# Down projections by seven block products beside a fixed order of the gate and up stage

## The chip, the core and the metric

The kernel runs on one core of a Trainium2 chip. The metric is the device time in microseconds of one execution. TensorE (PE) multiplies, VectorE (DVE) and ScalarE (ACT) split operands and take results out of PSUM, GpSimd (POOL) does some elementwise work and issues DMAs from a queue of its own, and SyncE (SP) issues the other DMAs.

## What is computed

Two layers over 768 tokens (256 of context, 512 latent) of 1024 features. Each layer is a SwiGLU half-step, a mixer, and a second SwiGLU half-step. In the second layer the context is needed up to the mixer's keys and values only, so that six sub-layers s = 0 to 5 run: SwiGLU on 768 tokens (s = 0, 2, 3), the two mixers (s = 1, 4), and SwiGLU on 512 tokens (s = 5).

```python
D_MODEL, SEQ, CTX_LEN, DEPTH, D_FF = 1024, 512, 256, 2, 2816

def _ffn_sublayer(h, shift, scale, gate, g_pre, g_post, w_gate, w_up, w_down):
    u = _modulate(_rmsnorm(h, g_pre), shift, scale)          # h * (1 + scale) + shift
    y = (jax.nn.silu(u @ w_gate) * (u @ w_up)) @ w_down
    return h + FFN_RES * gate * _rmsnorm(y, g_post)
...
for l in range(DEPTH):
    x  = _ffn_sublayer(x, ...);  xc = _ffn_sublayer(xc, ...)
    u  = _modulate(_rmsnorm(x, norm_pre[l, 1]), mod[:, 3], mod[:, 4])
    uc = _modulate(_rmsnorm(xc, norm_pre[l, 1]), mod_c[3], mod_c[4])
    y, yc = _even_mixer(...) if l % 2 == 0 else _odd_mixer(...)
    x = x + mod[:, 5] * _rmsnorm(y, norm_post[l, 1])
    x = _ffn_sublayer(x, ...)
    if not last: xc = the same for the context
return x
```

## The kernel before

**Products.** Every float32 product is made of three passes: an operand is split into hi (its leading bits, a copy by ACT) and lo (the rest, a subtraction by DVE), and hi*hi, hi*lo and lo*hi are accumulated in PSUM. `halves` (L191 to L196) makes the two parts; `weights` (L177) does so for a block of 1024 columns, 512 at a time.

**A SwiGLU sub-layer** (`ffn`, L527) works on two chunks of tokens, of n = 384 each for s = 0, 2 and 3. It has three parts.

- The first two of the 22 tiles of 128 features are plain products (`products`).
- *Gate and up*: the other twenty features, two tiles at a time, by seven products (`strassen`, L588; Strassen's scheme in Winograd's form). There are ten pairs p, each with a job for gate (b = 0) and one for up (b = 1), so twenty jobs. A job loads two blocks of weights, makes four sums of them on DVE (L614 to L617), splits seven blocks of 512 columns, and issues 84 matmuls of 384 columns (L601). ACT copies partial results out of PSUM (L629) and DVE adds (L634) and multiplies (L638). A pair of finished tiles h goes to DRAM (`hd`, L658).
- *Down*: `type2` (L665) per chunk c. For each of the 22 feature tiles it loads 1024 columns of the weights (L193 splits them) and 384 columns of h (`lhs`, L576, `hilo`, L721), and `t2mm` (L694) issues 18 matmuls of 512 columns for three tiles of 128 tokens (L701): three passes, two halves of D. The last four feature tiles (STAG = 4) are done token tile by token tile, 24 matmuls each, so that a token tile is finished while the next is still multiplied.

**The boundary** (`boundary`, L494). For a finished token tile, the squares (L505) and the product with the gate (L506) read PSUM. The rest, x += G * rms(y) (L514), the norm (`normed`, L407: L410, L414), the transposes on TensorE (`turned`, L416, L419) and the split of u (L395, L393, L193), is run at once for the second chunk, and for the first chunk beside the second chunk's products (`later`, L671). Where the next sub-layer uses seven products, `Sums` (L422) makes what they need of u; `prepare` (L430) has GpSimd add hi and lo of the first chunk again (L437).

**Order.** A scheduler puts the instructions of each engine in order, by the order of the program and a model of when operands are ready; each engine then runs its list strictly in order. `late` (L81) keeps an instruction behind those that were issued before it. s = 5 (`joint`) takes all four token tiles at a time in its down projection and is otherwise alike. The modulation (`ada_steps`, L104) runs step by step beside the jobs of s = 0 and the mixers.

## Time and profile before

| what | us |
|---|---|
| three runs | 2631.05, 2623.03, 2626.58 (median 2626.58) |
| span of the profiled execution | 2636.3 |
| TensorE busy, of this span | 2546.2 |
| VectorE busy | 1757.5 |
| ScalarE busy | 1351.8 |
| GpSimd busy | 325.3 |
| down projection of s = 0, first matmul to last of the first chunk | 392.8 to 485.3 |
| and of the second chunk | 485.1 to 582.4 |

The profiled execution is one run; its span is 9.7 us longer than the median of the runs. Matmuls are pipelined and overlap in the profile, so a busy TensorE says that matmuls are in flight, and the distance from one matmul to the next says how fast they go.

### The profile page before, as it was taken

How to read it: one execution, taken by the hardware profiler on the slowest of the kernel's cores; microseconds unless marked ns; L12 is line 12 of the kernel's file. 1: busy time of each engine (PE TensorE's matmuls, PEld its weight loads, DVE VectorE, ACT ScalarE, POOL GpSimd, SP SyncE). 2: the span in 40 equal slices, each digit the busy share in tenths (PEclk: the TensorE clock that was granted, in tenths of full speed). 3: DMA queues.
4: the chain of work that ended last, by engine and by line, in shares of the span. 5: the costliest groups of instructions: out<-in, count | busy, mean ns of one | idle time of the engine just before them, and what ended most of it. 6: DMA issues, size and time to landing. Idle time of an engine off the chain costs nothing.

```text
span 2636.3 us, 38740 instructions
## 1 busy us (share of the span) xinstructions
PE 2546.2 (97%) x13980; PEld 2237.5 (85%) x13980; DVE 1757.5 (67%) x3199; ACT 1351.8 (51%) x2783; POOL 325.3 (12%) x356
## 2 busy tenths in 40 slices
...
PEclk8999999999999999999999999999999999999999
DMA  7445436541387443232555332235554552544542
GB/s 275 144 160 168 152 127 206 192 160 53 119 293 266 157 141 96 96 105 100 187 184 189 124 97 95 98 107 177 198 181 152 200 176 82 177 135 128 161 167 88
DMA packets 147761, 403.00 MB, mean 153 GB/s; under 512 B 16504, under 2 KB 33576, under 8 KB 147568
## 3 DMA queue, kind: packets, MB, share of 16 engines
...
q14 instruction: 84, 0.69, 0.1%
HBM read 351.91 MB, written 48.55 MB: 152 GB/s over the span
## 4 chain that ended last, share of the span: by engine, by line
PE 80%; DVE 7%; issue 5%; ACT 3%; POOL 3%; DMA 2%; POOLq 0%; DVEq 0%; ACTq 0%; SPq 0%
PE px L601 17%; PE py L601 12%; PE pz L601 12%; PE d110a L701 4%; PE d100a L701 4%; PE d000a L701 4%; PE d010a L701 4%; PE ada L122 3%; PE d001a L701 3%; PE d101a L701 3%; PE eo0a L701 1%; PE oq1a L701 1%; PE qkv1a L701 1%; PE opT L1286 1%; PE gu L201 1%
## 5 line engine op out<-in xcount | busy, mean ns | idle before, releaser
L210 POOL TENSOR_TENSOR b_0pr<-b_0pv,mhalf 128x1 f32<-128x1 f32 x4 | 2.2, 560 | 983.9 <-DVE b_0pv L208 983.9
L634 DVE TENSOR_TENSOR cp<-px,cp 128x384 f32<-128x384 f32 (+1 forms) x160 | 76.5, 520 | 56.3 <-PE px L601 56.3
L724 ACT ACTIVATE hh<-hr 128x384 fp32r<-128x384 f32 x132 | 68.6, 521 | 81.5 <-DMA hr<-hd 80.6
L725 DVE TENSOR_TENSOR hh<-hr,hh 128x384 fp32r<-128x384 f32 x132 | 72.9, 559 | 50.6 <-ACT hh L724 49.5
L636 ACT ACTIVATE h<-cp 128x384 f32<-128x384 f32 (+1 forms) x160 | 77.0, 498 | 26.1 <-DVE cp L634 21.9
L122 PE MATMUL ada<-wa,sc 128*32 128x512 f32 x512 | 83.8, 611 | 0.5 <-DVE cols L137 0.4
L634 DVE TENSOR_TENSOR cp<-pz,cp 128x384 f32<-128x384 f32 (+1 forms) x80 | 41.9, 524 | 57.4 <-PE pz L601 56.4
L638 DVE TENSOR_TENSOR h<-cp,h 128x384 f32<-128x384 f32 (+1 forms) x160 | 79.6, 519 | 0.4
L629 ACT ACTIVATE cp<-px 128x384 f32<-128x384 f32 (+1 forms) x160 | 71.4, 446 | 0.0
L634 DVE TENSOR_TENSOR cp<-py,cp 128x384 f32<-128x384 f32 (+1 forms) x80 | 41.7, 521 | 26.7 <-PE py L601 17.2
L614 DVE TENSOR_TENSOR w<-w,w 128x512 f32<-128x512 f32 x80 | 56.8, 709 | 1.6 <-DMA w<-in_wgu_dram 0.2
L193 DVE TENSOR_TENSOR d110w_0lo<-d110w,d110w_0hi 128x512 fp32r<-128x512 f32 x22 | 15.2, 691 | 63.6 <-ACT d110w_0hi L193 63.6
L617 DVE TENSOR_TENSOR w<-w,w 128x512 f32<-128x512 f32 x80 | 55.3, 691 | 2.0
L615 DVE TENSOR_TENSOR w<-w 128x512 f32<-128x512 f32 x80 | 55.2, 690 | 1.9
L616 DVE TENSOR_TENSOR w<-w,w 128x512 f32<-128x512 f32 x80 | 55.1, 689 | 1.5
L701 PE MATMUL d011a<-d011w_0hi,hh 128*128 128x512 f32 x132 | 52.7, 399 | 0.2 <-ACT hh L724 0.2
L701 PE MATMUL d101a<-d101w_0hi,hh 128*128 128x512 f32 x132 | 52.5, 398 | 0.0
L701 PE MATMUL d001a<-d001w_0hi,hh 128*128 128x512 f32 x132 | 52.5, 398 | 0.0
L701 PE MATMUL d100a<-d100w_512hi,hh 128*128 128x512 f32 x132 | 52.4, 397 | 0.0
L701 PE MATMUL d000a<-d000w_512hi,hh 128*128 128x512 f32 x132 | 52.4, 397 | 0.0
L701 PE MATMUL d010a<-d010w_0hi,hh 128*128 128x512 f32 x132 | 52.3, 396 | 0.0
L701 PE MATMUL d101a<-d101w_512hi,hh 128*128 128x512 f32 x132 | 52.2, 396 | 0.0
...
## 6 DMA issues: line engine op xcount, KB each, us to landing
w<-in_wgu_dram SPq DMA_DIRECT2D x175, 512.0 KB, 3.5
...
wa<-in_w_ada_dram SPq DMA_DIRECT2D x42, 512.0 KB, 4.3
d000w<-in_w_down_dram SPq DMA_DIRECT2D x22, 512.0 KB, 3.5
d001w<-in_w_down_dram SPq DMA_DIRECT2D x22, 512.0 KB, 3.8
d010w<-in_w_down_dram SPq DMA_DIRECT2D x22, 512.0 KB, 3.9
```

The costliest lines, as they stand in the source:

```text
L122: ins = nc.tensor.matmul(acc[32 * g:32 * g + 32, :], lhsT=self.sc[:, k, :], rhs=raws[g], start=(k == 0), stop=(k == KD - 1), skip_group_ch ...
L601: mm = lambda x, y, **kw: nc.tensor.matmul(out, lhsT=x, rhs=y, skip_group_check=True, **kw)
L614: nc.vector.tensor_sub(x3, x1, x3)
L615: nc.vector.tensor_add(x1, x1, x2)
L617: nc.vector.tensor_sub(x4, x4, x2)
L629: nc.scalar.activation(t, src, AF.Copy)
L634: nc.vector.tensor_add(t, acc, t)
L636: nc.scalar.activation(hc, t, AF.Silu)
L638: nc.vector.tensor_mul(hc, t, hc)
L701: mm(acc[:, h:min(h + 512, n)], lhsT=x[xi][:, js], rhs=w[h // 512][wi], start=(k == 0 and xi == 0 and wi == 0), stop=(k == nk - 1 and xi = ...
L724: self.nc.scalar.activation(t[:, 0], src, AF.Copy)
L725: self.nc.vector.tensor_sub(t[:, 1], src, t[:, 0].bitcast(F32))
```

## The change

The change has five parts, for s = 0, 2 and 3 where nothing else is said.

1. *Down by seven products* (`down`). The features are taken as eleven pairs of tiles, the tokens as two chunks and D as two halves of 512. The sums of h (`h_sums`) and of the weights (`down_sums`) are made during gate and up and go to DRAM: `hd` has four blocks for a pair instead of two, and the new `wt` holds sums of the weights. `down_load` and `down_sums` load and store the weights on GpSimd's queue, in the two tiles that the gate uses later. `down` then runs seven products in turn, each over eleven feature tiles; loads and splits are made for two feature tiles at a time, four ahead (AHEAD). PSUM is taken out by `keep`, `left`, `right`, `right2` and `left2`.
2. *Gate and up in a fixed order*. `chain` ties each instruction of ACT and DVE in this stage (and of ACT, DVE and SP in `down`) to the one before it in the program. The weights of a job are made one job ahead, in the steps of the generator `made`. Splits are of 1024 columns, and the results of two chunks are taken in one instruction of 768 columns.
3. *The joint sub-layer* (s = 5) uses the same jobs without the fixed order; its down projection stays as it was.
4. *The boundary* is cut into halves of D and into two steps, norm (`rest`) and transposes (`make_u`), which are placed apart. `Sums.prepare` goes; the float32 tiles of u are kept.
5. *Storage*. Four slots of 1024 columns hold hi and lo, instead of eight of 512; blocks of 512 take a whole slot, too. The scratch for the DMAs of GpSimd's queue is set to 8192.

Cut to its core:

```diff
+    def chain(self, last, ins):
+        e = ins.ins.engine
+        if e in last:
+            self.tc.add_manual_dep(ins.ins, last[e], mybir.DependencyInfo(
+                mybir.DependencyClass.NoSync, mybir.DependencyReason.DATA), reason="chain")
+        last[e] = ins.ins.name
...
+    def wtiles(self, n, name, one=False):
+        return [self.ws.tile([P, n], F32R, tag=("o" if one else "w") + e, bufs=2 if one else 4, name=name + e) for e in ("hi", "lo")]
...
+        if sums is not None and c == 0:
+            ut = sums.first[j] = [self.c3([P, 4, P], F32, f"{name}b{h}") for h in range(2)]
...
-        def prepare(self):
...
+        def half(i, y):
+            nc.scalar.activation(self.junk(f"{name}{i}")[:, cut[i]], y, AF.Square, accum_out=ss[:, i:i + 1])
+            nc.vector.tensor_mul(y1[:, cut[i]], y, g[:, cut[i]])
+        def end():
+            nc.vector.tensor_add(ss[:, 0:1], ss[:, 0:1], ss[:, 1:2])
+            r = self.rms_r(ss[:, 0:1], D, name + "p")
+            def rest():
+                x = bp.tile([P, D], F32, tag="bx", bufs=2, name=name + "x")
+                nc.gpsimd.dma_start(x, xsrc(t))
...
+                    self.normed(x, y1, name + "u")
+            return rest, lambda: nxt and self.make_u(y1, t, *nxt, name + "u")
...
+    def down_load(self, l, s, p):
+        b = [self.bp.tile([P, D], F32, tag=f"G{e}", name=f"wt{l}{s}{p}{e}") for e in range(2)]
+        for e in range(2):
+            self.late(self.nc.gpsimd.dma_start(b[e], self.a["w_down"][l, s, (2 * p + e) * P:(2 * p + e + 1) * P, :]))
+        return b
+    def down_sums(self, b, wt, chain):
+        nc = self.nc
+        (b11, b12), (b21, b22) = ((x[:, 0:512], x[:, 512:]) for x in b)
+        chain(nc.vector.tensor_add(b11, b11, b12))
+        chain(nc.vector.tensor_add(b12, b12, b22))
+        self.late(nc.gpsimd.dma_start(wt[0], b[0]))
+        chain(nc.vector.tensor_add(b22, b11, b22))
+        chain(nc.vector.tensor_add(b21, b22, b21))
+        self.late(nc.gpsimd.dma_start(wt[1], b[1]))
+    def h_sums(self, h, n, hd, nm, joint, chain=lambda ins: ins):
+        nc = self.nc
+        a11, a21, a12, a22 = (x[:, c * n:(c + 1) * n] for x in h for c in range(2))
+        nc.sync.dma_start(hd[1], h[1])
...
+        s12 = self.bp.tile([P, 2, n], F32, tag="by", bufs=3, name=f"hs{nm}")
+        s4 = self.junk(f"hs{nm}")[:, 0:n]
+        chain(nc.vector.tensor_sub(s12[:, 0], a22, a21))
+        chain(nc.vector.tensor_sub(a21, a11, a21))
+        nc.sync.dma_start(hd[0], h[0])
+        minus = lambda out, x, y: chain(nc.vector.scalar_tensor_tensor(out, x, -1.0, y, op0=ALU.mult, op1=ALU.subtract))
+        minus(s12[:, 1], s12[:, 0], a11)
+        nc.sync.dma_start(hd[2], s12.rearrange("p c n -> p (c n)"))
+        minus(s4, s12[:, 1], a12)
+        nc.sync.dma_start(hd[3][:, 0:n], s4)
+    def down(self, l, s, n, hd, wt, g, start, finish, hook):
...
+        def make():
+            i, p, a, b = todo.pop(0)
...
+            w = min(2, np_ - p)
+            q = slice(p, p + w)
+            ar = self.c3([P, w, n], F32, f"dh{nm}")
+            chain(nc.sync.dma_start(ar, a(q)))
+            tag, bufs = ("bx", 2) if i < 5 and p // 2 % 3 == 2 else ("raw", 3)
+            br = self.ws.tile([P, w, 512], F32, tag=tag, bufs=bufs, name=f"dw{nm}")
+            chain(nc.sync.dma_start(br, b(q)))
+            ah, al = (self.c3([P, w, n], F32R, f"dh{nm}{e}") for e in "hl")
+            halves(ah, al, ar)
+            bh, bl = (t.rearrange("p (e n) -> p e n", e=w) for t in self.wtiles(w * 512, f"dw{nm}s"))
+            halves(bh, bl, br)
...
+        def run():
...
+            parts = {q: e for q, e in (((5, 0), (0, 0)), ((5, 2), (1, 0)), ((5, 6), (0, 1)), ((5, 7), (2, 0)), ((5, 9), (1, 1)), ((6, 1), (2, 1)))}
...
+                a = min(k + self.AHEAD, len(steps) - 1, (i + 1) * np_ + 1 if p > np_ - 4 else len(steps))
+                while todo and steps[a] not in ready:
+                    make()
...
+                end = np_ - (5 if i == len(jobs) - 1 else 3)
+                if p == 0 or end <= p < np_ - 1:
+                    continue
+                for j in range(m):
+                    for e in held:
+                        mms(acc[j], e, j, first)
+                    if p == np_ - 1:
+                        done(j, acc[j])
+                held = []
...
+            for xi, wi in ((0, 0), (0, 1), (1, 0)):
+                nc.tensor.matmul(out, lhsT=x[xi][:, js], rhs=w[wi], start=first and p == 0 and xi == wi,
...
+        def left(j, acc):
+            chain(nc.vector.tensor_add(k12[:, 0, j], acc, k12[:, 0, j]))
+            ends[0, j] = start(0, j, g)
+            ends[0, j][0](0, k12[:, 0, j])
+        def right(j, acc):
+            minus(k12[:, 1, j], acc)
+            ends[0, j][0](1, k12[:, 1, j])
+            finish(0, j, ends[0, j][1])
+        def right2(j, acc):
+            minus(u5[:, j], acc)
+            ends[1, j] = start(1, j, g)
+            ends[1, j][0](1, u5[:, j])
+        def left2(j, acc):
+            ends[1, j][0](0, acc)
+            finish(1, j, ends[1, j][1])
+        x, z = bank("dx"), []
+        product(blk(0, 0), raw(0, 0), x, True, keep(k12[:, 0]))
+        product(blk(1, 0), raw(1, 0), lambda: bank("dy"), True, left)
+        product(blk(2, 1), mod(1, 1), x, False, keep(k12[:, 1]))
+        product(blk(2, 0), mod(0, 0), lambda: z.extend(bank("dy")) or z, True, keep(u5))
+        product(blk(3, 0), raw(1, 1), lambda: z, False, right)
+        product(blk(0, 1), mod(0, 1), x, False, right2)
+        product(blk(1, 1), mod(1, 0), x, False, left2)
...
+        chain = (lambda ins: ins) if joint else lambda ins: self.chain(last, ins)
...
+            w["a11"], w["a12"] = cut(split(r1, nm + "a1"))
+            w["a22"] = split(r2[:, 512:], nm + "a22", True)
+            yield w
...
+            chain(nc.vector.tensor_sub(x3, x1, x3))
+            chain(nc.vector.tensor_add(x1, x1, x2))
+            chain(nc.vector.tensor_add(x2, x3, x2))
+            chain(nc.vector.tensor_sub(x4, x4, x2))
+            yield
+            w["s1"], w["s2"] = cut(split(r2, nm + "s12"))
+            yield
+            w["s3"], w["s4"] = cut(split(r1, nm + "s34"))
+            yield
...
+            (u1, u2), (u4, u5) = ([t[:, c] for c in range(2)] for t in cp)
+            product(x, w["a11"], b11, True)
+            copy(u1, x)
+            after = step()
+            product(y, w["a12"], b21, True)
+            chain(nc.vector.tensor_add(u1, y, u1))
+            step()
+            product(z, w["s1"], t1, True)
+            copy(u5, z)
+            product(x, w["s2"], t2, False)
+            copy(u2, x)
+            step()
+            product(z, w["s4"], b22, False)
+            chain(nc.vector.tensor_add(u2, z, u2))
+            out(0)
+            step()
+            product(y2, w["a22"], t4, True)
+            copy(u4, y2)
+            between()
+            product(x, w["s3"], t3, False)
+            chain(nc.vector.tensor_add(cp[1], x.unsqueeze(1).to_broadcast([P, 2, n]), cp[1]))
+            out(1)
...
+            if joint or (b and p != NF // 2 - 2):
+                return
+            r = p - 1 + b if p < NF // 2 - 1 else p
+            self.down_sums(wb, wt[r], chain)
+            if r < NF // 2 - 1:
+                wb = self.down_load(l, s, r + 1)
...
+        parts = dict(zip(range(1, 8), [(0, 0), (1, 0), None, (0, 1), (2, 0), (1, 1), (2, 1)] if len(ts) > 2 else
+                         [(0, 0), (1, 0), None, None, (0, 1), None, (1, 1)])) if ts else {}
...
+    nc = _bacc.Bacc("TRN2", target_bir_lowering=False, num_devices=1, dynamic_dma_scratch_size=8192)
```

**VectorE in gate and up of s = 2.** The rows are DVE's around the start of the job for p = 4, b = 0; names with 0140 are this job's weights, `cp01300` and the like the results of a job, `w` the loaded weights. Before:

```order
L193 TENSOR_TENSOR 0140a11lo_10461<-w01400_10456,0140a11hi_10460 128x512
L614 TENSOR_TENSOR w01400_10456<-w01401_10458,w01400_10456 128x512
L615 TENSOR_TENSOR w01401_10458<-w01401_10458 128x512
L193 TENSOR_TENSOR 0140a12lo_10465<-w01400_10456,0140a12hi_10464 128x512
L634 TENSOR_TENSOR cp01310_10354<-py00131_10350,cp01310_10354 128x384
L193 TENSOR_TENSOR 0140a22lo_10469<-w01401_10458,0140a22hi_10468 128x512
L638 TENSOR_TENSOR h01_6_10174<-cp01310_10354,h01_6_10174 128x384
L616 TENSOR_TENSOR w01401_10458<-w01400_10456,w01401_10458 128x512
L617 TENSOR_TENSOR w01400_10456<-w01400_10456,w01401_10458 128x512
L193 TENSOR_TENSOR 0140s1lo_10477<-w01401_10458,0140s1hi_10476 128x512
L193 TENSOR_TENSOR 0140s2lo_10481<-w01401_10458,0140s2hi_10480 128x512
```

After, where 0140 is made during the job before:

```order
L796 TENSOR_TENSOR 0140a1lo_9794<-w01400_9789,0140a1hi_9793 128x1024
L796 TENSOR_TENSOR 0140a22lo_9798<-w01401_9791,0140a22hi_9797 128x512
L846 TENSOR_TENSOR cp01310_9774<-py00131_9770,cp01310_9774 128x384
L809 TENSOR_TENSOR w01400_9789<-w01401_9791,w01400_9789 128x512
L810 TENSOR_TENSOR w01401_9791<-w01401_9791 128x512
L811 TENSOR_TENSOR w01401_9791<-w01400_9789,w01401_9791 128x512
L812 TENSOR_TENSOR w01400_9789<-w01400_9789,w01401_9791 128x512
L796 TENSOR_TENSOR 0140s12lo_9845<-w01401_9791,0140s12hi_9844 128x1024
L854 TENSOR_TENSOR cp01310_9774<-pz00131_9772,cp01310_9774 128x384
L839 TENSOR_TENSOR h01_6_9635<-cp01310_9774,h01_6_9635 128x768
L796 TENSOR_TENSOR 0140s34lo_9863<-w01400_9789,0140s34hi_9862 128x1024
L861 TENSOR_TENSOR cp01311_9775<-px00131_9773,cp01311_9775 128x768
```

The splits are wider, the two additions from py and pz stand at fixed places among them, and the multiplication of a feature tile is one row of 768 columns.

**VectorE from gate and up to down of s = 2.** The names `d010w` (before), `dh010` and `dw010` (after) are the down projection's operands; `cp01101` and `h01_20` belong to the last job. Before:

```order
L193 TENSOR_TENSOR 01101s4lo_12303<-w011010_12274,01101s4hi_12302 128x512
L193 TENSOR_TENSOR 01101s3lo_12307<-w011010_12274,01101s3hi_12306 128x512
L634 TENSOR_TENSOR cp011000_12176<-px001100_12175,cp011000_12176 128x384
L634 TENSOR_TENSOR cp011001_12177<-px001100_12175,cp011001_12177 128x384
L193 TENSOR_TENSOR d010w0_0lo_12428<-d010w0_12425,d010w0_0hi_12427 128x512
L193 TENSOR_TENSOR d010w0_512lo_12432<-d010w0_12425,d010w0_512hi_12431 128x512
L634 TENSOR_TENSOR cp011010_12314<-py001101_12310,cp011010_12314 128x384
L193 TENSOR_TENSOR d010w1_0lo_12461<-d010w1_12458,d010w1_0hi_12460 128x512
L638 TENSOR_TENSOR h01_20_12134<-cp011010_12314,h01_20_12134 128x384
```

After:

```order
L861 TENSOR_TENSOR cp011001_11528<-px001100_11526,cp011001_11528 128x768
L846 TENSOR_TENSOR cp011010_11656<-py001101_11652,cp011010_11656 128x384
L670 TENSOR_TENSOR dh010_0l_11779<-dh010_0_11774,dh010_0h_11778 128x768
L854 TENSOR_TENSOR cp011010_11656<-pz001101_11654,cp011010_11656 128x384
L839 TENSOR_TENSOR h01_20_11521<-cp011010_11656,h01_20_11521 128x768
L670 TENSOR_TENSOR dw010_0slo_11783<-dw010_0_11776,dw010_0shi_11782 128x1024
L861 TENSOR_TENSOR cp011011_11657<-px001101_11655,cp011011_11657 128x768
L670 TENSOR_TENSOR dh010_2l_11791<-dh010_2_11786,dh010_2h_11790 128x768
L839 TENSOR_TENSOR h01_21_11522<-cp011011_11657,h01_21_11522 128x768
L670 TENSOR_TENSOR dw010_2slo_11795<-dw010_2_11788,dw010_2shi_11794 128x1024
L639 TENSOR_TENSOR hs0110_11752<-h01_21_11522,h01_20_11521 128x384
L640 TENSOR_TENSOR h01_20_11521<-h01_20_11521 128x384
```

The first two feature tiles of the first product (`dh010_0`, `dw010_0`) are split ahead of the last job's final addition (`cp011011`), the next two behind it, and the sums of the last pair of h (`hs0110`) stand between the splits that follow.

**TensorE from down of s = 2 to the gate and up of s = 3.** The names `d011a` (before) and `dx012` (after) are the last token tile of the down projection, `b2_3utp` are the transposes of token tile 3, the first of the second chunk, and `gu1000` is the next sub-layer. Before:

```order
L701 MATMUL d011a2_13189<-d011w18_0hi_13900,hh011_18_13910 128x512
L701 MATMUL d011a2_13189<-d011w18_512hi_13904,hh011_18_13910 128x512
L701 MATMUL d011a2_13189<-d011w19_0hi_13915,hh011_19_13925 128x512
L701 MATMUL d011a2_13189<-d011w19_512hi_13919,hh011_19_13925 128x512
L419 MATMUL b2_3utp0_14006<-ident_66,b2_3y_13982 128x128 x4
L419 MATMUL b2_3utp1_14017<-ident_66,b2_3y_13982 128x128 x4
L701 MATMUL d011a2_13189<-d011w19_0lo_13916,hh011_19_13925 128x512
```

After:

```order
L729 MATMUL dx012_11773<-dw016_8slo_13076,dh016_8h_13071 128x512
L729 MATMUL dx012_11773<-dw016_8shi_13075,dh016_8l_13072 128x512
L729 MATMUL dx012_11773<-dw016_10shi_13105,dh016_10h_13101 128x512
L729 MATMUL dx012_11773<-dw016_10slo_13106,dh016_10h_13101 128x512
L729 MATMUL dx012_11773<-dw016_10shi_13105,dh016_10l_13102 128x512
L210 MATMUL gu1000_13316<-u3_0h_8756,w1000hi_13301 128x384
L211 MATMUL gu1000_13316<-u3_0l_8757,w1000hi_13301 128x384
L212 MATMUL gu1000_13316<-u3_0h_8756,w1000lo_13302 128x384
L210 MATMUL gu1000_13316<-u3_0h_8756,w1000hi_13301 128x384
L211 MATMUL gu1000_13316<-u3_0l_8757,w1000hi_13301 128x384
L212 MATMUL gu1000_13316<-u3_0h_8756,w1000lo_13302 128x384
L210 MATMUL gu1000_13316<-u3_0h_8756,w1000hi_13301 128x384
L435 MATMUL b2_3utp0_13146<-ident_66,b2_3y_12936 128x128 x4
```

The transposes of token tile 3 stood 17 matmuls ahead of the end of the down projection and now stand seven matmuls behind it.

## Rows read from the trace of the kernel before

**Rows 1.** The page: busy time of each engine, and the shares of TensorE and DMA in 40 slices.

```profile
PE 2546.2 (97%) x13980; PEld 2237.5 (85%) x13980; DVE 1757.5 (67%) x3199; ACT 1351.8 (51%) x2783; POOL 325.3 (12%) x356
PEclk8999999999999999999999999999999999999999
DMA  7445436541387443232555332235554552544542
GB/s 275 144 160 168 152 127 206 192 160 53 119 293 266 157 141 96 96 105 100 187 184 189 124 97 95 98 107 177 198 181 152 200 176 82 177 135 128 161 167 88
```

**Rows 2.** Stages: start:end, length, busy time of each engine (count), PEclk, DMA share, GB/s.

```profile
392.70:484.80 92.10, 92.10 (x396) 74.23 (x395) 48.87 (x86) 42.35 (x82) 2.08 (x3) 1.00 0.59 193
485.00:582.00 97.00, 95.72 (x427) 77.18 (x427) 55.00 (x125) 47.80 (x99) 16.97 (x24) 1.00 0.55 183
992.00:1272.00 280.00, 280.00 (x1617) 280.00 (x1616) 192.71 (x323) 135.26 (x253) 0.00 (x0) 1.00 0.32 103
1506.00:1800.00 294.00, 294.00 (x1666) 294.00 (x1665) 198.95 (x334) 139.45 (x262) 0.00 (x0) 1.00 0.30 100
```

**Rows 3.** Pieces of the chain that ended last: start us, length us, engine, tile, line, count.

```profile
392.84 92.41 PE d000a L701 x396
493.66 5.59 PE d001a L701 x24
...
1008.74 4.16 PE px L601 x24
1023.30 4.16 PE px L601 x24
...
1520.05 4.24 PE px L601 x24
...
2023.89 7.71 PE okv1a L701 x33
```

**Rows 4.** Groups of instructions by line and form: VectorE, 992 to 1272 us.

```profile
L634 DVE TENSOR_TENSOR cp<-px,cp 128x384 f32<-128x384 f32 x38 | 19.4, 553 | 17.1 <-PE px L601 17.1
L617 DVE TENSOR_TENSOR w<-w,w 128x512 f32<-128x512 f32 x18 | 12.5, 693 | 0.6
L193 DVE TENSOR_TENSOR 0120s2lo<-w,0120s2hi 128x512 fp32r<-128x512 f32 x1 | 0.7, 693 | 1.1 <-ACT 0120s2hi L193 1.1
```

**Rows 5.** The same view: VectorE, 1272 to 1500 us.

```profile
L514 DVE SCALAR_TENSOR_TENSOR b_0x<-b_0y,b_0pr,b_0x 128x1024 f32<-128x1024 f32 x1 | 1.3, 1286 | 0.7 <-POOL b_0pr L210 0.7
```

**Rows 6.** The same view: ScalarE, 1272 to 1500 us.

```profile
L505 ACT ACTIVATE b_3q<-d011a 128x512 f32<-128x512 f32 x2 | 1.2, 598 | 5.4 <-PE d011a L701 4.7 <-DVE b_3y L506 0.8
L410 ACT ACTIVATE b_2y<-b_2x 128x1024 f32<-128x1024 f32 x1 | 1.1, 1064 | 3.5 <-DVE b_2x L514 3.5
```

**Rows 7.** VectorE in order of time within one job; in brackets idle before and what ended it.

```profile
1063.40 0.69 DVE L193 TENSOR_TENSOR 0140s2lo<-w,0140s2hi 128x512 fp32r<-128x512 f32 x1 [1.07 <-ACT 0140s2hi L193]
1065.01 0.56 DVE L634 TENSOR_TENSOR cp<-pz,cp 128x384 f32<-128x384 f32 x1 [0.92 <-PE pz L601]
```

**Rows 8.** Waits of TensorE: waiter and line <- releaser, us in total, times, longest.

```profile
PE b_5utp L419 <- POOL b_5y L414: 8.0, 4, 3.2
PE b_4utp L419 <- POOL b_4y L414: 7.9, 5, 2.4
PE b_3utp L419 <- POOL b_3y L414: 3.8, 4, 0.9
PE oq1a L701 <- DVE oq1w_512lo L193: 1.7, 1, 1.7
```

**Rows 9.** DMA issues on the page: tile, queue, count, size, median us to landing.

```profile
w<-in_wgu_dram SPq DMA_DIRECT2D x175, 512.0 KB, 3.5
```

**Rows 10.** The list of all DMA issues: loads and stores of the GpSimd queue.

```profile
G<-gd POOLq DMA_DIRECT2D x10, 512.0 KB, 4.3
xd<-b_4x POOLq DMA_DIRECT2D x5, 512.0 KB, 3.3
```

**Rows 11.** Groups on GpSimd over the span: the additions of `prepare`.

```profile
L437 POOL TENSOR_TENSOR b<-u_0h,u_0l 128x512 f32<-128x512 f32 x16 | 25.8, 1628 | 7.9 <-DVE u_0l L193 7.1 <-PE b_3utp L419 0.4 <-PE b_2utp L419 0.4
```

276 lines of the change are left out of this document (163 added, 113 removed).

## The prediction

> **What bounds the kernel now.** I read the page first: TensorE has matmuls in flight for 2546.2 of 2636.3 us, 97% [rows 1]. Busy time alone does not say that it is fed, so the stages come next. In the first chunk of a down projection its busy time equals the window (92.10 of 92.10 us), as it does in gate and up (280.00 of 280.00), while VectorE is at 53% and 69% there, and the granted clock is 1.00, the level of 2.4 GHz [rows 2]. The chain of waits then shows that nothing stands between the matmuls: 396 of them in 92.41 us, that is 0.2333 us each, and two jobs of gate and up start 14.56 us apart, which is 84 matmuls at 0.1733 us (4.16 us for 24) [rows 3]. So in these stages the time is the count of matmuls times a fixed step, and only fewer matmuls shorten them. The waits of TensorE that a row names are small; the largest stand before the transposes of the boundary, 8.0 + 7.9 + 3.8 = 19.7 us over the five boundaries [rows 8].
>
> **The change part by part.** *Down by seven products.* Before, a sub-layer has 6 token tiles x 22 feature tiles x 3 passes x 2 halves = 792 matmuls of 512 columns. After, it has 7 products x 3 token tiles x 11 feature tiles x 3 passes = 693. The order confirms 2079 rows against 2376 for the three sub-layers. The 297 that go are worth 297 x 0.2333 = 69.3 us. The new stage writes one PSUM bank several times in a row where the old one alternates between two; the nearest row for that is the key and value projection of s = 4, 33 matmuls in 7.71 us, 0.2336 us each [rows 3], so the step stays.
>
> A row contradicts a rule here. The Trainium skill (TensorE: Matmul & The Clock Gate, section Back-to-back issue gap) gives about 216 ns for a lone warm matmul of 512 columns and 131 ns in a sustained stream. The trace has 233 ns. By the skill's two figures the term would be 64 or 39 us; the measured step decides.
>
> *What feeds the new down stage.* For two feature tiles of a product TensorE takes 18 x 0.2333 = 4.2 us. VectorE makes the lo parts of 768 and 1024 columns. No row of before has a split of 1024; an operation of 1024 columns takes 1.29 us [rows 5] and one of 512 takes 0.69 [rows 4], which puts 768 at 0.99 as an estimate. That makes 2.3 of 4.2 us. ScalarE needs about as much (1024 columns: 1.06 us [rows 6]). Taking out a product's PSUM adds at most three additions and three gate multiplications, 4.1 us of VectorE in 23.1. Both engines stay behind TensorE.
>
> *Entry into that stage.* By the order the first two feature tiles are split before the last job ends, so TensorE starts at once with 4.2 us of work. Behind the last product VectorE has an addition of 768 columns (0.99), a split (0.99), a multiplication (0.99) and a split (1.29), 4.3 us, before the next two tiles are ready. The stall is 0 to 1.5 us; I take 0.5, for three entries +1.5 us.
>
> *Gate and up in a fixed order, with the new sums.* Matmuls stay as they are, so this is worth nothing unless VectorE falls behind. A job has three splits of 1024 columns (3.9 us), one of 512 (0.7), four sums of weights (2.8), two additions of 384 columns (1.1 at 0.553 [rows 4]) and one of 768 (1.0): 9.4 us. A pair of jobs has 18.8, and 2.0 for the multiplications, 2.2 for the sums of h and 2.8 for those of the down weights: 25.8 us. The same durations give 21.9 us for a pair before, where VectorE was really busy for 192.71 / 280 x 29.12 = 20.0 [rows 2], since neighbours overlap; by that share it is 23.6. On top come the waits for ScalarE that a fixed order can't fill, once in each job a split of 1024 columns (1.06) and in the gate job Silu and another split, at most 2.1: 4.2 us. A pair then takes VectorE 27.8 to 30.0 us, and TensorE 29.12. What is made is used late: the last weights of a job are wanted in its fifth product, four products or 8.3 us after the job's start, so VectorE may slip 0.83 us a pair over ten pairs before TensorE notices. The limit is 29.95 us. I take 0, with the cover nearly used up. Behind VectorE's waiting instruction everything in the chain is queued, splits for TensorE included; that is the first rival.
>
> *DMAs of the stage.* The queue of GpSimd gets two loads and two stores of 512 KB a pair. A store takes 3.3 us and a load 4.3 us to land [rows 10]; the next pair's sums come 29.1 us later (14.6 for the last two pairs), so they are hidden. On SP's queue two more stores a pair stand in front of weights that are wanted a job later (a load of weights lands in 3.5 us [rows 9]). No cost.
>
> *The boundary.* For the second chunk half of D is taken out one product earlier, so a square (0.60 us [rows 6]) and a multiplication leave the chain behind the last matmul. Against that the token tiles end 15 x 0.2333 = 3.5 us apart instead of 5.6 (24 matmuls in 5.59 us [rows 3]), and by the order the transposes of the first tile stand seven matmuls behind the end instead of 17 ahead of it, with as much time since its own last matmul. The named waits may vanish or double (19.7 us either way over the five); I take 0. `prepare` goes, 16 additions of 1.63 us on GpSimd [rows 11], which matters where GpSimd's norm is waited for: 0 to -4 us, I take -1.5.
>
> *Slots.* The 512-column weights of the key and value projection have four slots instead of eight, so a following product may wait for its first split. The nearest row is the 1.7 us that a query product waited for one [rows 8]; at two places 0 to 3.4, I take +1.
>
> *Step of gate and up.* 24 matmuls take 4.16 us in s = 2 and 4.24 in s = 3 [rows 3]; I know no reason, and placement of operands changes. A switch is worth 0.08 / 24 x 1680 = 5.6 us a sub-layer: -11 to +6, I take 0.
>
> The sum is -69.3 + 1.5 - 1.5 + 1.0 = -68.3 us on the profiled span of 2636.3, so 2568. That execution was 0.37% longer than the median of the runs (2626.58); scaled, 2558 us.
>
> **The rivals.** *The fixed order holds TensorE.* Each us that a pair takes VectorE beyond 29.95 costs 10 us a sub-layer, 30 in all. For it: the idle time of VectorE before is partly waiting for ScalarE (1.07 us ahead of one split) and partly for TensorE (0.92 ahead of an addition) [rows 7], and a fixed order fills neither. At 31 us a pair the time is 2558 + 31 = 2589. If all of that idle time stays, (280 - 192.71) / 280 x 29.12 = 9.1 us a pair, a pair takes 23.6 + 9.1 = 32.7 us and the kernel 2558 + 82 = 2640, slower than before; the side changes at (68 / 3 + 8.3) / 10 = 3.1 us above 29.12, 32.2 us. Against it: VectorE runs behind TensorE by then, and the waits for TensorE are gone.
>
> *DMA holds the down stage.* A product loads 11 x (192 + 256) KB = 5.05 MB. At the 193 GB/s of before [rows 2] seven take 183 us, where 792 matmuls took 185: nothing gained, 2621 us. Needed are 218 GB/s, a share of 0.59 x 218 / 193 = 0.67, and about 286 with the boundary's x in the last two products. Against it: one slice has 293 GB/s at a DMA digit of 8 [rows 1].
>
> *The sums of the down weights come late.* The order makes VectorE wait for each load on GpSimd's queue. The change of side is at a round trip of about 32 us, where the two rows give 7.6 [rows 10]. At five times that, 38 us, VectorE would wait 8 us a pair, and the kernel would take some 2800. The Trainium skill (SBUF — State Buffer, section SBUF: two separate sides) has such a mechanism: certain VectorE operations lock GpSimd out of a shared port, so that it cannot write the descriptors of its DMAs, and it gives 0.62 against 3.1 us for one transfer. No row here shows such a delay, and by the page it is copies within SBUF that do it, not additions of two operands.
>
> That the matmuls do not go is excluded by the order.
>
> **How the numbers follow.** Forecast, TensorE bound throughout: 0.78, 2542 to 2574 (the step -11 to +6, the boundary about 10 either way, entry and slots +3). Fixed order with a moderate stall, up to 2600: 0.10. Fixed order past the turning point: 0.05. DMA bound: 0.04. Late sums: 0.02; the boundary or something unseen, still faster: 0.01. The range holds 8 in 10 if it reaches from 2542 into the moderate stall, 2588. Runs of this kernel differ by about 0.3%, 8 us, which is what a measurement can tell from no change. Faster by more: 0.78 + 0.10 + 0.01 = 0.89; within: 0.04 for the DMA case and 0.01 from the edge of the stall; slower: 0.06.
>
> **What would show it.** Right: 693 matmuls of 512 columns in some 162 to 167 us in each of the three down stages, jobs of s = 2 still about 14.6 us apart, waits before the boundary's transposes near 20 us in total. Fixed order: jobs further apart than 14.8 us, and TensorE waiting for a split. DMA: splits in the down stage that wait for `hd` or the weights. Late sums: VectorE waiting in gate and up for a load of the down weights. The forecast is wrong if any of these reaches 20 us, or if the step of the new matmuls is above 0.24 us.

## The result, and the profile after

The changed kernel takes 2596.96 us (median of 4 runs, 2593.1 to 2600.38) against 2628.39 us before: a ratio of 0.988, 95% interval 0.9858 to 0.9901. It is 31 us faster, 1.2%; 2558 us, 68 less, was forecast, and 2597 lies above the range, which ended at 2588. The direction was right, the size was not: less than half of the gain arrived.

The page of the changed kernel, the lines that answer [rows 1]: busy time of the engines, then the shares in 40 slices.

```profile
PE 2489.6 (96%) x13683; PEld 2188.9 (84%) x13683; DVE 1877.6 (72%) x2946; ACT 1290.7 (50%) x2346; POOL 373.3 (14%) x472
PEclk8999999999999999999999999999999999999999
DMA  7677767651387435555776355558764652544552
```

The 297 matmuls are gone (13980 to 13683), VectorE has 120 us more, and the clock's row of digits is the same. The next view gives two stages of the changed kernel, columns as in [rows 2]: down of s = 0 from the first of its seven products into the fifth, and gate and up of s = 2.

```profile
404.80:500.00 95.20, 95.20 (x408) 76.69 (x409) 58.29 (x89) 51.86 (x71) 3.21 (x6) 1.00 0.75 261
974.30:1270.10 295.80, 295.80 (x1680) 295.80 (x1680) 237.93 (x319) 123.73 (x184) 23.53 (x44) 1.00 0.56 197
```

And pieces of its chain of waits, as in [rows 3]:

```profile
414.86 23.10 PE dy L729 x99
437.96 23.10 PE dx L729 x99
...
1001.95 4.24 PE px L784 x24
...
1016.75 4.24 PE px L784 x24
```

In the middle of down all is as forecast: 99 matmuls in 23.10 us are 0.2333 us each, and TensorE never waits, though the DMA engines now carry 261 GB/s at a share of 0.75. In gate and up it does not wait either; 24 matmuls take 4.24 us, the longer of the two values of [rows 3], and two jobs start 14.80 us apart. The rest of the loss must be at the edges of stages. To find it, the kernel before was profiled a second time (the first experiment below), because the execution behind [rows 1 to 11] was long: 2636.3 us, where the second has 2621.3. Against the second, the changed kernel's span (2591.3) is 30.0 us shorter, as the medians say. The distances between the first matmuls of the stages, in us, with "down" reaching to a fixed place behind the boundary (the first gate product of the recurrence, the first of the seven-product jobs, the first query product):

| stretch | before, again | after | change | forecast |
|---|---|---|---|---|
| down s = 0 and boundary | 227.7 | 211.4 | -16.3 | |
| down s = 2 and boundary | 233.0 | 216.2 | -16.8 | -69.3 for the three |
| down s = 3 and boundary | 229.8 | 213.7 | -16.1 | (and entries +1.5, prepare -1.5) |
| gate and up, s = 2 | 291.2 | 296.0 | +4.8 | 0 |
| gate and up, s = 3 | 291.2 | 295.9 | +4.7 | 0 |
| gate and up, s = 0 and 5 | 513.6 | 511.3 | -2.3 | 0 |
| s = 1: product ga0 | 8.5 | 17.1 | +8.6 | |
| s = 1: the rest of the mixer | 311.2 | 310.1 | -1.1 | +1.0 for all |
| plain products of s = 2 | 40.9 | 45.7 | +4.8 | |
| s = 4, queries to gate and up | 261.5 | 264.5 | +3.0 | |
| opening, last down, last boundary | 212.8 | 209.6 | -3.2 | 0 |
| span | 2621.3 | 2591.3 | -30.0 | -68 |

The three down stages gave 49 us, not 69, and a net 19 us of that were lost in gate and up and in the mixers.

The waits of TensorE by row, as in [rows 8], of the changed kernel:

```profile
PE b_5utp L435 <- POOL b_5y L430: 5.9, 3, 2.5
PE ga0a L210 <- ACT ga0w0hi L203: 5.7, 1, 5.7
...
PE b_4utp L435 <- POOL b_4y L430: 5.4, 4, 2.2
...
PE gu L212 <- DVE w0110lo L203: 4.3, 1, 4.3
...
PE xaa L210 <- DVE b_4pv L218: 3.0, 1, 3.0
PE b_3utp L435 <- POOL b_3y L430: 2.8, 4, 0.9
PE gu L210 <- DVE b_3uv L218: 2.7, 1, 2.7
...
PE dx L729 <- ACT dw_6shi L669: 2.6, 3, 1.7
...
PE okv0a L935 <- DVE b_5y L514: 2.0, 1, 2.0
```

The waits that the forecast named, before the transposes, fell from 19.7 to 14.1 us. But the first product behind each down stage (xaa, gu, okv0a) now waits for VectorE, 3.0 + 2.7 + 2.0 us, where the kernel before had no such wait; together that is 21.8. Waits for weights in the first mixer and in the plain products behind it (ga0w0hi, w0110lo) are new as well.

### The profile page after: what moved, and what is told of

The parts are those of the page before. It is cut to its first block, busy times and chain, and to the rows that moved or that the text cites. A ratio compares the mean times of both kernels' runs of the same rounds, so it can differ in the third digit from the quotient of the medians.

```text
span 2591.3 us, 36846 instructions
## 1 busy us (share of the span) xinstructions
PE 2489.6 (96%) x13683; PEld 2188.9 (84%) x13683; DVE 1877.6 (72%) x2946; ACT 1290.7 (50%) x2346; POOL 373.3 (14%) x472
## 3 DMA queue, kind: packets, MB, share of 16 engines
q0 software_dynamic: 29888, 107.74, 11.7%
## 4 chain that ended last, share of the span: by engine, by line
PE 78%; DVE 7%; issue 7%; DMA 3%; ACT 3%; POOL 2%; SPq 0%; POOLq 0%; DVEq 0%; ACTq 0%
PE px L784 18%; PE py L784 12%; PE pz L784 12%; PE dy L729 8%; PE dx L729 5%; PE d11a L935 5%; PE ada L129 3%; PE oq1a L935 1%; PE gu L211 1%; PE gu L212 1%; PE eo0a L935 1%; PE gu L210 1%; PE qkv1a L935 1%; DMA dw<-in_w_down_dram 1%; PE pT L1332 1%
## 5 line engine op out<-in xcount | busy, mean ns | idle before, releaser
L837 ACT ACTIVATE h<-cp 128x768 f32<-128x768 f32 (+1 forms) x80 | 63.3, 792 | 195.7 <-DVE cp L861 138.8
L831 ACT ACTIVATE cp<-pz 128x384 f32<-128x384 f32 (+1 forms) x80 | 37.0, 463 | 87.2 <-PE pz L784 87.0
L861 DVE TENSOR_TENSOR cp<-px,cp 128x768 f32<-128x768 f32 (+1 forms) x80 | 70.8, 884 | 5.1 <-PE px L784 5.0
L839 DVE TENSOR_TENSOR h<-cp,h 128x768 f32<-128x768 f32 (+1 forms) x80 | 71.2, 891 | 2.2
L613 POOL DMA_DIRECT2D wt<-in_w_down_dram x66 | 35.5, 537 | 113.1 <-DMA wt<-wt 113.1
L1324 POOL TENSOR_SCALAR p<-p,sm 128x256 f32<-128x256 f32 (+2 forms) x48 | 31.9, 677 | 136.3 <-DVE sm L1321 63.1
L670 DVE TENSOR_TENSOR dw_0slo<-dw,dw_0shi 128x1024 fp32r<-128x1024 f32 x21 | 25.7, 1225 | 25.6 <-ACT dw_0shi L669 25.3
L831 ACT ACTIVATE cp<-py 128x384 f32<-128x384 f32 (+1 forms) x80 | 36.3, 454 | 14.3 <-PE py L784 13.9
L1223 ACT ACTIVATE optb<-opT 128x512 fp32r<-128x512 f32 x48 | 28.6, 597 | 28.3 <-PE opT L1520 27.9
L1511 POOL TENSOR_SCALAR op<-op,osm 128x768 f32<-128x768 f32 x32 | 30.6, 956 | 75.8 <-DVE osm L1510 53.4
L1223 ACT ACTIVATE ptb<-pT 128x512 fp32r<-128x512 f32 x44 | 26.3, 597 | 30.3 <-PE pT L1332 29.9
```

What stands on the lines that cost most here:

```text
L831: chain(nc.scalar.activation(t, src, AF.Copy))
L837: chain(nc.scalar.activation(hc, cp[f], AF.Silu))
L839: chain(nc.vector.tensor_mul(hc, cp[f], hc))
L861: chain(nc.vector.tensor_add(cp[1], x.unsqueeze(1).to_broadcast([P, 2, n]), cp[1]))
L1223: self.nc.scalar.activation(b[:, n, 0], tp, AF.Copy)
```

## The experiments

Ratios are to the kernel before, with 95% intervals; the changed kernel has 0.988.

**e_before.** No edit.

> The kernel before, unchanged, for a second profile of it. Between the two profiles the change took 45 us off (2636.3 to 2591.3), between the medians 31 (2628.4 to 2597.0). If the first profile of before was a long execution, this one has a span near 2626 us and the difference lies in a few stretches that both profiles have. Two readings of the step of gate and up (0.1767 us a matmul in s = 3, 0.1733 in s = 2): if it belongs to where the operands lie, it stands at 296.6 us for s = 3 and 291.0 for s = 2 again; if it belongs to the single execution, s = 3 comes out near 291 or s = 2 near 296.

Measured: 2626.2 us, ratio 0.9999 (0.9981 to 1.0016); span 2621.3. Gate and up took 291.2 us in both s = 2 and s = 3, so the step of one and the same program in the same stage was 0.1767 us in one execution and 0.1733 in the other. It belongs to the execution there. This row of the second profile stands against the 294.00 of [rows 2], which did not hold the whole stage:

```profile
1504.00:1795.20 291.20, 291.20 (x1682) 291.20 (x1681) 201.85 (x338) 141.74 (x266) 0.00 (x0) 1.00 0.30 102
```

**e_nochain.** The fixed order of gate and up is taken away:

```diff
-        chain = (lambda ins: ins) if joint else lambda ins: self.chain(last, ins)
+        chain = lambda ins: ins
```

> The changed kernel without the fixed order in gate and up (the fixed order of the down projection stays). My account of the lost time has nothing in gate and up: its stretch of s = 2 and s = 3 was 296 us, 0.1762 us a matmul, without a wait. By it the stretches stay at 295 to 297 us and the kernel at 2597, give or take 5. Rival, the fixed order holds TensorE in a way that the waits do not name: the stretches fall to 291 us and the kernel to about 2585. Third case, the fixed order is what makes the new sums fit: the stretches grow, by 10 us or more each, and the kernel is above 2625.

Measured: 2686.8 us, ratio 1.0222 (1.0206 to 1.0238): the third case of the expectation. Gate and up took 348.4, 318.7 and 319.3 us in s = 0, 2 and 3: 82 us more than with the fixed order. The stage, a wait of TensorE in it, and an instruction of VectorE:

```profile
1021.60:1340.10 318.50, 303.46 (x1680) 300.27 (x1680) 231.23 (x317) 126.65 (x184) 21.36 (x40) 0.98 0.52 183
...
PE pz L784 <- ACT cp L831: 13.0, 5, 3.7
...
1060.42 0.69 DVE L621 TENSOR_TENSOR wt<-wt 128x512 f32<-128x512 f32 x1 [3.58 <-DMA wt<-in_w_down_dram]
```

The scheduler puts the sums of the down weights where their load has not landed, VectorE stands 3.6 us, and the results behind it come late. In this stage VectorE stands so nine times, 21.1 us in all, and TensorE takes 22.7 us longer; with the fixed order VectorE has no such wait and does much the same work (237.9 us in the stage) without holding TensorE. My first rival is turned round: the fixed order is not the danger, it is what makes the sums fit. The fixed order that `down` has for ACT, DVE and SP was not lifted in any run.

**e_olddown.** The down projection of before, sums left out, the rest of the change kept:

```diff
-        self.down(l, s, n, hd, wt, self.load_gate(*gate), start, finish, hook)
+        for c in range(2):
+            self.type2(f"d{l}{s}{c}", NF, lhs, len(tiles[0]), ..., fin, hook=hook if c == 1 else None)
```

> The changed kernel with the down projection of before (792 matmuls a sub-layer, the sums of h and of the down weights are left out, 24 matmuls a token tile at the end instead of 15), with everything else of the change. From the first matmul of down to the same place behind the boundary, before took 227.7, 234.4 and 229.8 us in s = 0, 2 and 3, the changed kernel 211.4, 216.2 and 213.7: 50.7 saved where 69.3 were expected from the matmuls. Theory of the tail: what is lost comes with the shorter tail of the new down projection, the boundary itself is no slower; the three stretches return to within 2 us of before and the kernel takes about 2634 (before and 6 us for the mixers). Rival, the boundary in two steps is slower in itself: the stretches are 4 to 6 us longer than before each, and the kernel takes about 2648.

Measured: 2667.4 us, ratio 1.0152 (1.0137 to 1.0167). The stretches are 231.8, 252.3 and 230.7 us: 4.1 and 0.9 more than before in s = 0 and 3, and 19 more in s = 2, where TensorE waits 11.7 us for h, whose loads stand behind those of weights on SP's queue. The mixers and gate and up are as slow as in the changed kernel (ga0 17.3, plain products of s = 2 45.7, 295.8 us), so these losses do not come from the seven products. For the boundary the run is between the two readings. From the first squares to the last tile's transposes it takes 25.8, 31.0 and 24.8 us, where the kernel before takes 25.5, 30.9 and 26.4 and the changed one 21.4, 27.0 and 20.9: with the old down the new boundary is no quicker in s = 0 and 2.

**e_tail9 and e_tail21.** The tail of the last product, over which the token tiles end one by one ("squares" are the first operations of a token tile's norm, here on the half of D that is finished last; for 21 the last feature tile also goes to a narrow slot):

```diff
-                end = np_ - (5 if i == len(jobs) - 1 else 3)
+                end = np_ - 3
...
+                end = np_ - (7 if i == len(jobs) - 1 else 3)
```

> The changed kernel with the last of the seven products finished token tile by token tile over three feature tiles instead of five: 9 matmuls of 512 columns (2.1 us) a token tile instead of 15 (3.5 us). From the first matmul of down to the same place behind the boundary the changed kernel takes 211.4, 216.2 and 213.7 us in s = 0, 2 and 3. Theory of the tail: norm and transposes of the first token tile take a fixed 8.8 us, and the matmuls of the two tiles behind it are what covers them; with 2 x 1.4 us less cover each stretch grows by 2 to 3 us and the kernel by 6 to 9 (2605). Rival, the boundary waits for something else (loads of x, the throughput of VectorE): the stretches stay within 1 us and the kernel at 2597.

> The other way: seven feature tiles at the end, 21 matmuls (4.9 us) a token tile, and the single last feature tile of a product takes its hi and lo from the narrow slots, so that three wide slots are held at the end as before. Theory of the tail: 2 x 1.4 us more cover, each of the three stretches shrinks by 2 to 3 us (to about 209, 213.5 and 211) and the kernel by 6 to 9 (2589). Rival, the slots decide: the feature tiles held back keep slots from the weights of the next sub-layer, and what the tail gives is lost at its first products; the stretches stay or grow.

Measured: 2602.2 (0.9904, 0.9881 to 0.9927) and 2602.9 us (0.9907, 0.9886 to 0.9927); stretches 212.0, 216.6, 216.0 and 209.7, 218.0, 217.0. Neither tells anything of the tail: in both, and in the changed kernel, the last matmul of down begins 3.8, 3.3 and 3.8 us after the squares of the first token tile (before: 12.8). The program asks for 9, 15 or 21 matmuls a token tile in a row; the scheduler interleaves the tiles, and some 8 stand in a row in all three.

**e_force15 and e_force21.** The same tail, tied to the program's order:

```diff
+                if tail:
+                    self.chain(tailed, mm)
```

> The changed kernel with the matmuls of the last product's end tied to the program's order, 15 in a row for each token tile. In the runs so far, those with 9 and 21 included, the last matmul of down came 3.8, 3.3 and 3.8 us after the squares of the first token tile began (before: 12.8): the scheduler interleaves the token tiles and only some 8 matmuls a tile stand in a row, whatever the program says. So the length of the tail has not been varied yet. Here the distance is about 6.6 us. Theory of the tail: the three stretches fall by up to 2.8 us each, to about 209, 214 and 211, and the kernel takes 2589. Rival, the three token tiles pass through the other engines one behind the other and take 21 us or more in any case, or TensorE now waits for the last feature tile: the stretches stay within 1 us or grow.

> The same with seven feature tiles at the end, 21 matmuls in a row for each token tile, the single last feature tile in a narrow slot: the last matmul of down about 9.4 us behind the first squares. Theory of the tail: up to 5.6 us less for each stretch, 206 to 208, 211 to 213 and 208 to 210, and the kernel 2580 to 2585. Rival as before: the stretches stay within 1 us, or the slots that are held to the end keep the next weights back and they grow.

Measured: 2605.9 (0.9910, 0.9876 to 0.9945) and 2606.1 us (0.9903, 0.9874 to 0.9931). Now the last matmul begins 9.0 and 11.1 us after the first squares (s = 0), and the stretches are 213.0, 219.8, 214.8 and 212.0, 221.0, 214.5: no shorter. The theory of the tail falls. The first squares do come 1.9 to 3.9 us earlier; with 15 in a row the last transposes, too, come 2.4 and 2.5 us earlier in s = 0 and 2, but TensorE has stood 5.3 and 6.9 us behind the end of down and has 23 and 36 more instructions left behind them.

**e_banks.** The PSUM banks of the down projection exchanged:

```diff
-        x, z = bank("dx"), []
+        y0, x, z = bank("dy"), bank("dx"), []
...
-        product(blk(1, 0), raw(1, 0), lambda: bank("dy"), True, left)
+        product(blk(1, 0), raw(1, 0), y0, True, left)
```

> The changed kernel with the two groups of three PSUM banks of the down projection exchanged. Between the last matmul of down and the first of what follows, the changed kernel has 3.35, 3.11 and 2.41 us in s = 0, 2 and 3, before had 0.2. Theory of the banks: the first accumulator of the next sub-layer lies over the banks of the last product, so its first matmul waits until VectorE has read the last token tile (in s = 0 that multiplication ended at 560.38 and the matmul began at 560.43); over the other group, which is long free, the gap is 0.2 to 0.3 us, the stretches from the first matmul of down to behind the boundary fall from 211.4, 216.2 and 213.7 by 2 to 3 us each, and the kernel takes 2589. Rival, u of the second chunk decides: the matmuls of the first chunk start earlier and then stand longer before the transposes; the stretches stay within 1 us.

Measured: 2598.1 us, ratio 0.9878 (0.9860 to 0.9895), stretches 211.5, 216.4 and 213.9. The rival holds. Waits of TensorE between 555 and 600 us, first of the changed kernel, then of this one:

```profile
PE xaa L210 <- DVE b_4pv L218: 3.0, 1, 3.0
PE b_3utp L435 <- POOL b_3y L430: 0.9, 1, 0.9
...
PE b_3utp L435 <- POOL b_3y L430: 4.2, 1, 4.2
```

The wait in front of the first matmul is gone, and the transposes wait that much longer.

**e_late and e_latebanks.** The transposes of the second chunk are put behind 48 to 96 of the next products' matmuls, in the second kernel with the banks exchanged:

```diff
-                for f in parts:
-                    f()
+                parts[0]()
+                if s in (0, 1, 2, 4):
+                    self.pend.append(parts[1])
+                else:
+                    parts[1]()
```

> The changed kernel with the transposes of the second chunk's token tiles placed later in TensorE's order where gate and up or the recurrence follow: not 3 to 10 matmuls behind the end of the products, but behind the first chunk's first 48 matmuls (the last of them behind all 96; before the recurrence behind 72). Theory of the place: norm and split of the last token tiles take about 18 us from the last matmul on, the first chunk's matmuls could cover 12 to 17 of it, and the transposes that stand in front of them make TensorE wait instead; then the 7.8 and 9.6 us of waits behind the last matmul in s = 0 and 2 fall by 2 to 4 each, the 3 us for the PSUM banks stay, and the kernel takes 2588 to 2592. Rival, the chain up to the split of the last tile is what counts: the waits only move to the second chunk's first matmul, and the stretches stay within 1 us.

> The same with the PSUM banks exchanged. If both theories hold, the exchange is now worth its 3 us, since the first chunk's matmuls start at once and no transposes stand in front of them: the stretches of s = 0 and 2 fall to 205 to 207 and 209 to 212 us and the kernel takes 2582 to 2587. If the chain up to the split decides, the exchange is worth nothing here either, and the kernel takes 2594 or more.

Measured: 2617.2 (0.9953, 0.9934 to 0.9973) and 2612.7 us (0.9937, 0.9913 to 0.9960): worse than the changed kernel. In s = 2 the stretches are 217.0 and 223.5 us. In s = 0 the second has 205.5, but only because the first gate product now stands ahead of matmuls that it used to follow: up to ga0 it takes 225.9 us instead of 220.5. The waits move on, to ScalarE's part of u: in the second kernel 1.9 us for u_1h in s = 0, and in s = 2 5.0 us before the second tile's transposes and 2.2 for u_1h.

**e_entry.** The sums of the last pair of h, with their stores, are moved behind the first feature tiles of down:

```diff
+                if k == 2:
+                    self.h_sums(tail, n, hd[np_ - 1], f"{l}{s}{np_ - 1}", False, chain)
```

> The changed kernel with the sums of the last pair of h, and their stores, moved from the end of gate and up behind the first feature tiles of the down projection. The waits in the first 25 us of down were 1.5, 3.6 and 2.3 us in s = 0, 2 and 3 against none before. Theory of the queue: the loads of the fourth pair of feature tiles stand on SP's queue behind four stores of these sums (in s = 2 issued at 1278.5, while the slot was free from about 1271.5); with the stores moved the waits fall to 0.3 to 1 us each and the kernel by 5 (2592). Rival, the slots of the loaded weights and the time to land (4 to 6 us) set it: the waits stay within 1 us of what they were.

Measured: 2594.3 us, ratio 0.9862 (0.9845 to 0.9879). The waits in the first 25 us of down fall from 1.5, 3.6 and 2.3 us to 1.3, 1.5 and 1.2, by 3.4 us in all, and the down stages as wholes become 0.1, 1.4 and 1.1 us shorter. In the changed kernel SP's queue shows the store of the last sum right ahead of the load:

```profile
1278.10 0.32 SPq L646 DMA_DIRECT2D hd<-hs0110q  x1
1278.51 0.41 SPq L685 DMA_DIRECT2D dh<-hd  x1
```

The theory of the queue holds for part of the wait in s = 2 and 3; what stays is more than the 0.3 to 1 us that it expected, and in s = 0 next to nothing changes. The kernel's gain of 3 us is too small for such runs to tell.

**e_slots, e_whole and e_five.** Three ways to get the second half of ga0's weights split in time, in this order in the diff: blocks of 512 in the narrow slots; one instruction for the whole block; five wide slots instead of four and two narrow ones (with the edit of e_entry).

```diff
-    ... for ts in [self.wtiles(n, name)] ...
+    ... for ts in [self.wtiles(n, name, n <= 512)] ...
...
+        self.halves(ts[0], ts[1], raw)
...
+        return [self.ws.tile([P, n], F32R, tag="w" + e, bufs=5, name=name + e) for e in ("hi", "lo")]
```

> The changed kernel, but blocks of 512 columns take their hi and lo from the two narrow slots that only gate and up uses, not from the four of 1024 columns. Theory of the slots: in s = 1 the first gate product (ga0a, 48 matmuls) took 16.95 us instead of 8.14 because the gate weights of the recurrence (gw, 512 columns) occupy whole slots, so that the second half of ga0w is split behind ScalarE's activations; here it takes 8 to 9 us and the kernel 8 us less than the changed kernel (2589). Rival, the order of ScalarE: the split stands behind the activations for another reason; ga0a stays near 17 us and the kernel at 2597.

> The changed kernel, but a block of weights is split by one instruction of ScalarE and one of VectorE for all its columns, not 512 at a time. In the changed kernel the second half of ga0w was split 16 us after the first, behind eleven activations. Theory, it is the second half that is left behind: with one instruction there is none; the products of ga0 to ga3 take 43 to 45 us instead of 52.1 (before: 43.1) and the kernel 2588. Rival, as with the narrow slots the wait only moves to a later product: the four still take 50 us or more and the kernel 2597 or above.

> The changed kernel with five slots of 1024 columns for everything in place of four and two narrow ones (the same storage), and the sums of the last pair behind the first feature tiles of down. Theory of the slots: with a fifth slot both halves of ga0w are split before the activations, ga0 to ga3 take 43 to 48 us instead of 52.1, and nothing waits longer for it elsewhere. Second question, the step of gate and up: in every trace of the changed kernel the sixth product of a job, whose weights lie in a narrow slot, runs at 0.1734 us a matmul and the others at 0.1767. If the place of that block sets the step, all seven products now have one step, and s = 2 and s = 3 take 291.2 us if it is 0.1733, or 296.8 if it is 0.1767. With both gains and the entries the kernel takes 2578 to 2583; with the slots and the entries alone 2587; if the scheduler gives all of it away elsewhere, 2594 as with the entries alone.

Measured: 2599.8 (0.9894, 0.9880 to 0.9909), 2597.2 (0.9880, 0.9859 to 0.9902) and 2594.5 us (0.9853, 0.9837 to 0.9870). ScalarE, first in the changed kernel, then with five slots:

```profile
601.51 0.63 ACT L203 ACTIVATE ga0w0hi<-ga0w 128x512 fp32r<-128x512 f32 x1 [5.28 <-PE xaa L211]
604.28 3.28 ACT L1036 ACTIVATE lr<-lg,gb 128x768 f32<-128x768 f32 x4
...
617.84 0.61 ACT L203 ACTIVATE ga0w0hi<-ga0w 128x512 fp32r<-128x512 f32 x1
...
604.07 0.63 ACT L203 ACTIVATE ga0w0hi<-ga0w 128x512 fp32r<-128x512 f32 x1 [2.05 <-PE xaa L211]
605.40 0.64 ACT L203 ACTIVATE ga0w0hi<-ga0w 128x512 fp32r<-128x512 f32 x1
```

In the changed kernel the first half is split when a product gives up its slot, and the second lands behind the activations. In all three kernels ga0 takes 8.4 us again, but the time from its end to the query, key and value product rises from 35.0 to 42.5, 39.3 and 39.9 us (in the first of the three TensorE now waits 4.7 us for ga2's weights), and more is lost elsewhere (9.9 us in the opening with five slots, 6.4 in the boundary of s = 2 with whole blocks). Five slots also answer the second question, below.

**e_bslots.** The slots alone, in the kernel before:

```diff
-        return self.ws.tile([P, n], F32R, tag="w" + s, bufs=8, name=name + s)
+        return self.ws.tile([P, n], F32R, tag="w" + s, bufs=4, name=name + s)
```

(and pairs of blocks share a slot of 1024).

> The kernel before with one part of the change alone: four slots of 1024 columns for hi and lo instead of eight of 512, and a block of 512 takes a whole slot. Theory of the slots: the losses of the mixers come from this part; ga0a takes 17 us instead of 8.4, the first plain products of s = 2 take 45.6 instead of 41, and the query projection of s = 4 about 69 instead of 66; if the layout of the slots also sets the step, gate and up of s = 2 and s = 3 take 296 instead of 291.2. The kernel then takes 2645 to 2660 (gate and up has one block less in flight as well). Rival, the order that the scheduler makes from the boundary in two steps: ga0a stays at 8.4, the mixers as before, and the kernel within 5 us of 2629.

Measured: 2675.1 us, ratio 1.0178 (1.0154 to 1.0202). ga0 takes 17.5 us: the slots alone make this loss. The stretch from the first query product of s = 4 to the first transposes of its attention takes 70.8 (65.8 before), the plain products of s = 2 41.6 (40.9), so most of the 4.8 us there is not the slots' doing. Another 28 us lie in s = 1's attention, where my edit also halved the room for the modulation's weights; the total says nothing of the change. Gate and up took 296.8 in s = 2 and 291.2 in s = 3: wide slots alone do not fix the step.

**e_banksentry, e_all and e_lateall.** Banks and sums together; the weights of the recurrence in one instruction too; late transposes besides.

> Both of the edits before this: banks exchanged, sums of the last pair moved. If each holds by itself and nothing else moves, the three stretches are about 207.5, 210.5 and 210 us and the kernel takes 2584. Rival, every edit lets the scheduler put the splits of the mixers elsewhere, and what is gained at the boundary is lost there: 2590 or more, with other stretches longer than in the changed kernel.

> The same with the weights of the recurrence's products (xa, ga0 to ga3) split in one instruction each, as in the kernel that split all weights so, but nowhere else. If the gains add, ga0 to ga3 take 44 to 48 us instead of 52.1 and the kernel 2579. Rival as before: the gain is lost at a later product, and the kernel takes as long as with the two edits alone.

> Late transposes, exchanged banks, the sums of the last pair behind the first feature tiles, and the weights of the recurrence split in one instruction each. If the gains add (2 to 4 us each at two or three boundaries, 3 at the two banks, 4 at the entries, 4 to 6 at the gates) the kernel takes 2572 to 2582. If what is gained at one place is waited for at the next, 2588 or more.

Measured: 2595.0 (0.9869, 0.9849 to 0.9890), 2593.7 (0.9860, 0.9842 to 0.9879) and 2598.7 us (0.9884, 0.9853 to 0.9915). In e_all ga0 to ga3 take 45.9 us instead of 52.1, and what follows, up to the output projection, 2.5 more. The gains do not add. None of these kernels can be told from the changed one.

## Why the prediction was wrong, and where it was right

**The term that was mis-sized: 297 x 0.2333 = 69.3.** Count and step are right; that all of these matmuls lie on the path is not. The chain of waits at the end of down in s = 0, first of the kernel before, then of the changed one:

```profile
559.78 9.81 PE d001a L701 x42
569.62 0.70 ACT b_3q L505 x2
...
593.29 1.81 POOL b_5y L414
595.16 1.09 PE b_5utp L419 x8
```

```profile
544.87 8.41 PE dx L729 x36
553.31 0.70 ACT b_30q L513 x2
...
558.14 3.15 DMA xd<-b_3x
...
572.84 1.81 POOL b_5y L430
574.70 1.09 PE b_5utp L435 x8
```

In both kernels the path leaves TensorE when the first token tile of the second chunk is finished, runs through norm after norm on four engines and a store, and comes back with the last tile's transposes. The rest of down runs beside it: 48 matmuls before (12.8 us from the first squares to the last matmul), 16 after (3.8 us; a little less in s = 2). So of the 99 matmuls that a sub-layer lost, 32 stood beside the chain; by the step they would be 22.4 us in the three stages. Split at the first squares, the stretches add up:

| us | to the first squares: before, after | from there on: before, after |
|---|---|---|
| s = 0 | 176.9, 163.2 | 50.7, 48.1 |
| s = 2 | 178.3, 166.7 | 54.7, 49.5 |
| s = 3 | 177.0, 164.0 | 52.8, 49.7 |
| change | -38.2 | -11.1 |

The first column lost 67 matmuls a stage, 3 x 67 x 0.2333 = 46.9 us, less 7.4 for the entries and 1.3 more. The second fell by 11.1 us only. It is the way to the last tile's transposes, for which TensorE waits, and what TensorE then has left:

| us | first squares to last transposes: before, after | behind them: before, after |
|---|---|---|
| s = 0 | 25.5, 21.4 | 25.2, 26.7 |
| s = 2 | 30.9, 27.0 | 23.8, 22.5 |
| s = 3 | 26.4, 20.9 | 26.4, 28.8 |
| change | -13.6 | +2.5 |

The last split of u, the profile before again and after:

```profile
596.99 1.29 DVE L193 TENSOR_TENSOR u_1l<-b_5uut,u_1h 128x512 fp32r<-128x512 f32 x2 [0.40 <-ACT u_1h L193]
```

```profile
577.60 1.29 DVE L203 TENSOR_TENSOR u_1l<-b_5uut,u_1h 128x512 fp32r<-128x512 f32 x2 [0.40 <-ACT u_1h L203]
```

It ends 29.7 and 25.6 us after the first squares, and TensorE reaches the second chunk's products 0.2 and 1.4 us after that, straight from matmuls of the first chunk: the split is ready just in time, and the transposes are what is waited for. That explains the banks: the waits of TensorE moved, the last transposes came within 0.4 us of where they came before the edit, counted from the first squares, and nothing was gained. With the tail forced, earlier squares were paid for by a longer chain (21 in a row: 26.1, 30.1 and 24.7 us) or by more matmuls left behind it (15 in a row, s = 0 and 2).

The chain did get shorter in the changed kernel, by 3.9 to 5.5 us, and that is what the second column gained. The boundary in two steps did not do it in s = 0 and 2, as e_olddown shows, nor did the end of `prepare` in s = 0 and 3, where the kernel before has none. So most of it came with the new down, whose token tiles end closer together and of which half of D is out earlier; which of the two did it was not tried apart. Nor did any run shorten the chain alone: that it holds the end of down is read from the traces, and the edits around it agree. TensorE's granted clock also fell to 0.50, the level of 1.2 GHz, for 3.4 us at each of the three boundaries, 1.3 to 2.2 us after the first product had begun behind its new wait of 2.4 to 3.4 us; before, it stayed at 1.00 in s = 0 and 3 and fell once in s = 2. What that cost was not separated from the waits around it, the next transposes' above all.

The step that failed is the paragraph on the boundary: it compared how far the token tiles end apart and took 0, so that all 297 matmuls counted in full. The runs show 11.1 us for the 96 beside the chain in place of 22.4, and 56.7 in place of 69.3 for the whole term (49.3, and the 7.4 that the entries took). The paragraph also had the distance wrong (15 matmuls, 3.5 us; the trace has some 8), and rested on the 19.7 us of named waits, which measure what TensorE lacked, not what the chain takes.

Against the second profile of before 30.0 us were gained where 68.3 were forecast. Of the 38.3 us between, the boundaries account for 11.3 and the 1.3 of the first column, the entries for 5.9, the step of gate and up for 9.5, ga0 and the plain products of s = 2 for 13.4 where 1.0 was allowed, and `prepare` for the 1.5 that it was to give; the small changes elsewhere in the table gave 3.6 back.

**Entry.** 0.5 us a stage was forecast, 1.5, 3.6 and 2.3 came, for the reason that e_entry shows in part: the stores of the last sums stood ahead of the loads on SP's queue. I had named that queue for gate and up only. The down stages took 167.0, 170.0 and 167.8 us from the first matmul to the last, where 162 to 167 was to be the sign of a right forecast.

**Gate and up.** A pair of jobs was to keep VectorE 23.6 us busy; it did 237.93 / 10 = 23.8, and TensorE did not wait. The rivals of the fixed order and of the late sums did not come about; e_nochain shows the mechanism of the late sums, VectorE held by a load and TensorE behind it, in the order without the tie. The Trainium skill's account of a port that keeps GpSimd from its DMAs (SBUF — State Buffer, section SBUF: two separate sides) has no sign here: 66 loads of the down weights landed in 4.6 us (median) beside a VectorE that was busy 80% of the time. What cost 9.5 us was the step: I allowed for a switch of 5.6 a sub-layer either way and took 0, and both stages came out near the upper level. Against the first profile, from which I forecast, s = 3 was there already.

**Slots.** +1 us was forecast, up to 3.4, from a wait for a first split. ga0 alone cost 8.6, shown by e_bslots to be the slots' and by e_whole and e_five to be the second half left behind ScalarE's activations. The waits are 5.7 and 0.8 us of it. The remaining 2 us or so come behind them: from 618.5 to 623.0 the granted clock is 0.50, and matmuls that began 0.177 us apart begin 0.32 apart. The 4.8 us of s = 2's plain products are a split of w0110 that stands on VectorE behind the last tile's x; they appear with the old down projection too and, but for 0.7 us, not with the slots alone, so they may belong to the new boundary or to what the scheduler makes of it; not settled.

**DMA.** The down stage moves 261 GB/s, more than the 218 that I had called necessary, and behind the entry TensorE is busy throughout. That rival fell. The end of the kernel, 3.5 us shorter, I had not seen; the last token tile now leaves in halves, which would explain it.

**The matmul's price.** By the two figures of the Trainium skill (TensorE: Matmul & The Clock Gate, section Back-to-back issue gap) the term would be, as an estimate, 39 or 64 us. The gain of the three stages, 49, falls between, but by accident: the trace has 0.2333 us again, and it is the count on the path that was smaller.

The forecast's chances went wrong in the same place: 0.10 was given to a moderate stall of the fixed order, up to 2600, and 0.78 to TensorE bound throughout, though the chain of waits of before already left TensorE for 25 us at the end of down in s = 0.
